# First feed-forward output layer: 18 instead of 16 of 22 hidden rows in seven-product pairs

## Chip, cores and metric

The kernel runs on one core of one Trainium2 chip. The metric is the device time of one execution in microseconds (us); lower is better. The engines named are TensorE (PE, matrix products), VectorE (DVE) and ScalarE (ACT) for elementwise work, GpSimd (POOL) for elementwise work off the matrix accumulators, and SyncE (SP), whose queue issues most of the DMA transfers. PSUM is the accumulator memory that PE writes; it is held here in banks named `mm` (four), `pn` (one) and `aux` (three).

## What is computed

The reference is one inference step of a one-layer decoder for 1024 prompt tokens and 8 sample tokens (1032 columns in the kernel, where activations stand transposed: features on the partitions, tokens along the row). The part that matters is the first of its two feed-forward networks and what follows it:

```python
def swiglu(x, wi, wo):
    g, u = jnp.split(x @ wi, 2, axis=-1)
    return (jax.nn.silu(g) * u) @ wo
...
x = layer_norm(ALPHA * x + 0.5 * swiglu(x, ffn1_wi, ffn1_wo), ln_g[0], ln_b[0])
z = x @ w_in + b_in
```

The model width is 1024, the hidden width 2816, that is 22 hidden rows of 128 features (pairs 0 to 10 of two rows). `ffn1_wo` is 2816 x 1024. A second network (`ffn2`), built by the same function with its own places, runs near the end.

## The kernel before

**Products.** Each float32 operand is split in two parts, high and low (`hilo`, `wload`, `wcomb`: a copy on ACT, then a subtraction on VectorE), and a product is three matmuls: high by high, high by low, low by high. A *plain* unit (`unit`, lines 172 to 174) makes one output tile of 128 features for one block of columns. A *seven-product* segment (`product`, lines 432 to 434) takes a 2 x 2 block product (two hidden rows by two output tiles, and the two halves of the columns) with seven products instead of eight; the sums that this needs of the weights (`wcomb`: two on VectorE, two on POOL) and of the activations are made beside the matmuls. The 1032 columns are two halves of 516, each in a part of 256 and one of 260: four blocks, numbered 0 to 3; blocks 0 and 2 have 256 columns, 1 and 3 have 260 (`BLK4`).

**Hidden layer.** `ffn` first makes pair 0 by plain units, then pairs 1 to 10 in seven products (`hidden`, `pair`). `spill` writes a pair to DRAM: for a pair that the output layer takes plainly, the two rows as they are (`hscr`); for one that it takes in seven products, the seven combinations of half-rows (`hsum`), for which it makes four sums on VectorE and four on POOL (lines 514 to 517).

**Output layer.** `groups` lists which pairs go together through the segments and, for each of the seven products, which places in SBUF hold their half-rows. For each group the half-rows are loaded from `hsum` by SP and split (`split_load`: cast on ACT, line 588; subtraction on VectorE, line 589); then four segments follow, one for each 256 output features. A segment loads its part of `ffn1_wo`, makes the seven weight combinations (lines 258 to 275), runs 7 products x 2 column parts x the group's pairs x 3 matmuls, and adds each product to the result rows `RT` (line 612, VectorE, from PSUM). Before: the groups are the pairs (1, 2, 3), (4, 5, 6) and (7, 8).

`plains` lists the rows that remain, each with two places. Before: rows 0, 1, 18, 19, 20, 21 (pairs 0, 9 and 10). Their activations come from `hscr` by the same `split_load`, the six 128 x 1024 weight rows by `wrow` in two halves (lines 148 and 149: cast on ACT, subtraction on VectorE) into 12 places: the nine of the weight ring and three `extra` ones.

**Tail and norm.** The plain rows are not multiplied at once. `tail1` only hands on the result rows and a function `last`, which the code after `ffn` calls for each block in the order 0, 2, 1, 3 and each of eight output tiles: one plain unit over all plain rows, then an addition to the result row (line 647, VectorE, high priority). `ln_sum` adds up the block on POOL (lines 369 and 371), and `ln_halves` makes the norm: a matmul with a matrix of 1/1024 for the mean (line 385), eight subtractions from PSUM on VectorE (390), eight squares on ACT (392), their sum on POOL and VectorE (396 to 404), a second matmul for the variance (407), the reciprocal root on ACT and its refinement on VectorE (409 to 412), then scale on VectorE (415), shift on ACT (417), and the high and low parts of the result (211 and 212). From the second block on, the first VectorE step queues behind the root of the block before. So each block's norm runs while PE makes the next block's units. Units take PSUM from `mm` and `pn` in turn, five in all.

After that the q and k projections are made by plain units for the four blocks in the same order, 96 matmuls a block, evicted by ACT (line 976). Meanwhile VectorE and POOL make the sums of x for the seven-product projections (lines 222 to 225, split at 211 and 212) and the first weight combinations, and the first pair of projections begins.

**Order.** Each engine works through its own queue in order. The order within a queue comes from the build: a scheduler takes the program's operations by priority and readiness, so moved places and other dependencies change the order in the queues too. A place in SBUF (numbers 0 to 35, the ring's names and `sreg`) is reused when all readers of its last content are done; a transfer into a place that isn't free waits at the head of SP's queue.

Of the kernel before, what the change touches and what calls it, by code (L numbers as in the profile page):

```python
# [63 lines left out]
def layer_kernel(ctx: ExitStack, tc: tile.TileContext, I, O):  # L64
# [12 lines left out]
    def gen(i, dt=F32, n=NT):  # L77

        tag = f"a{i}" if isinstance(i, int) else i
        return sb.tile([128, 1024 if tag in WN else 4 * BM], dt, name=tag, tag=tag)[:, :1024 if tag in WN else n]  # L80
# [56 lines left out]
    def set_ring(slots):  # L137
        ring["slots"] = slots
        ring["i"] = 0

    def wload(src, k, n, dst=None, raw=None, eng=None):

        if raw is None:
            raw = rawp.tile([128, 512], F32, name="raw", tag="raw")[:, :k * n]
            DQ.dma_start(raw.rearrange("p (k n) -> p k n", n=n), src)
        s = slot() if dst is None else dst
        hi, lo = s[:, :k * n], s[:, 512:512 + k * n]
        S.copy(hi, raw)
        (eng or V).tensor_tensor(lo, raw, F_(hi), op=OP.subtract)  # L149
        return hi.rearrange("p (k n) -> p k n", n=n), lo.rearrange("p (k n) -> p k n", n=n)  # L150
# [12 lines left out]
    def wrow(w, rows, half, dst=None):  # L163

        t = [wload(w[r:r + 128, half * 512:(half + 1) * 512].rearrange("p (k n) -> p k n", n=128), 4, 128,
                   gen(dst[i], R) if dst else None) for i, r in enumerate(rows)]
        return [[(hi[:, j, :], lo[:, j, :]) for hi, lo in t] for j in range(4)]
# [15 lines left out]
    def bs(t, b, blk=BLK):  # L183
        c0, n = blk[b]
        return t[:, c0:c0 + n]
# [95 lines left out]
    xscr = tc.dram_tile([8, 128, NT], F32, name="xscr")  # L281
# [202 lines left out]
    def ffn(wi, wo, l, XS, enter, xlate, raws, sgs, RTs, res, groups, plains, tail, extra=None):  # L484
# [99 lines left out]
        def split_load(t, src):  # L584

            hi, lo = t
            DQ.dma_start(F_(lo), src)
            S.copy(hi, F_(lo))
            V.tensor_tensor(lo, F_(lo), F_(hi), op=OP.subtract)  # L589
            return hi, lo  # L590
# [51 lines left out]
        def ounit(js, w, m, b, blk=BLK):  # L642
            ps = unit_ps(blk[b][1])
            unit(ps, w, cols([hid[j][0] for j in js], [hid[j][1] for j in js], b, blk))
            r = bs(RT[m], b, blk)
            with tc.high_priority():
                V.tensor_tensor(r, r, ps, op=OP.add)  # L647

        for gi, rows_ in enumerate(plains):
            js = [j for j, _ in rows_]  # L650
            for j, ss in rows_:
                hid[j] = split_load([gen(x, R) for x in ss], hscr[j])
            rows = [j * 128 for j in js]
            if gi < len(plains) - 1:
                for half in range(2):
                    ws = wrow(wo, rows, half)
                    for q in range(4):
                        for b in range(3):
                            ounit(js, ws[q], half * 4 + q, b)
            else:  # L660
                if extra:
                    r = ring["slots"][ring["i"] % 9:] + ring["slots"][:ring["i"] % 9]
                    set_ring(r)
                    ws = wrow(wo, rows, 0, r[0:5] + extra[0:1]) + wrow(wo, rows, 1, extra[1:] + r[5:])
                else:
                    ws = wrow(wo, rows, 0) + wrow(wo, rows, 1)
                tail(RT, lambda m, b, blk: ounit(js, ws[m], m, b, blk))
# [47 lines left out]
    def xlate1():  # L715
        tslot(X1[0], 0, (16, 20, 8, 12))
        tslot(X1[0], 1, (17, 21, 9, 13))
        for kp in range(4):
# [2 lines left out]

    G1 = [((1, 2, 3), (0, 1, 2, 3, 4, 5, 6, 7, 14, 15, 22, 23, 8, 9, 10, 11, 12, 13, 26, 27, 28)),
          ((4, 5, 6), (29, 34, 35, 0, 1, 2, 3, 4, 5, 6, 7, 14, 15, 22, 23, 8, 9, 10, 11, 12, 13)),
          ((7, 8), (34, 35, 26, 27, 28, 29, 0, 1, 2, 3, 8, 9, 10, 11))]
    T1 = [list(zip((0, 1, 18, 19, 20, 21), ((4, 5), (6, 7), (14, 15), (22, 23), (12, 13), (34, 35))))]
    RT1 = []

    def tail1(RT, last):
        RT1.extend(RT)
        RT1.append(last)  # L730

    ffn(I["ffn1_wi"][0], I["ffn1_wo"][0], 0, X1, enter1, xlate1, [30, 31, 32, 33], [14, 15, 34, 35],
        [16, 17, 24, 25, 18, 19, 20, 21], xscr, G1, T1, tail1, [28, 29, 33])


    w_in = I["w_in"][0]
# [753 lines left out]
    for m in range(8):  # L1490
        for b in range(3):
            ps = unit_ps(BLK[b][1])
            unit(ps, wa[m // 4][m % 4], cols(MH[:K2], ML[:K2], b))
            r = bs(r2[m], b)
            V.scalar_tensor_tensor(r, r, ALPHA, ps, op0=OP.mult, op1=OP.add)
    rows = [k * 128 for k in range(K2, 8)]
# [57 lines left out]
    def tail2(RT, last):  # L1554
# [3 lines left out]
        for b in range(4):  # L1558
# [14 lines left out]
          ((7, 8, 9), (30, 31, 32, 35, 4, 5, 0, 1, 6, 7, 2, 3, 28, 29, 33, 34, 10, 11, 12, 13, 25))]  # L1573
    T2 = [[(0, (14, 15))], [(1, (30, 31)), (20, (32, 33)), (21, (24, 25))]]
    ffn(I["ffn2_wi"][0], I["ffn2_wo"][0], 2, X2, enter2, xlate2, [16, 17, 26, 27], [33, 34, 8, 9],
        (21, 22, 23, 18, 19, 20, 8, 9), rscr, G2, T2, tail2)

# [252 lines left out]
```

## Time and profile before

| | us |
|---|---|
| median of three runs | 2691.29 (2688.82 to 2695.84) |
| profiled execution, whole | 2685.85 |
| its span, first to last instruction | 2684.0 |
| PE busy in the span | 2638.3 |
| VectorE busy | 1871.4 |
| ACT busy | 1287.8 |
| POOL busy | 652.8 |

The output layer of the first network begins at about 466 us of the span. The second group starts at 525, the third at 587; the tail's units begin at 624, the q and k units at 697, and the first projection pair at 745 us. A window row of the profile gives, for one stretch, its length, then the busy time of PE, weight loads, VectorE, ACT and POOL with the number of instructions after x, then the granted PE clock, the DMA share and the rate. A group row gives line, engine, operation, what it writes and reads, the count, the busy time and the mean of one in ns, and after the bar the idle time of the engine just before these instructions and who ended it. A waits row reads: who waited, for whom, us in total, how often, the longest.

### The profile page before, as it was taken

How to read it: one execution, taken by the hardware profiler on the slowest of the kernel's cores; microseconds unless marked ns; L12 is line 12 of the kernel's file. 1: busy time of each engine (PE TensorE's matmuls, PEld its weight loads, DVE VectorE, ACT ScalarE, POOL GpSimd, SP SyncE). 2: the span in 40 equal slices, each digit the busy share in tenths (PEclk: the TensorE clock that was granted, in tenths of full speed). 3: DMA queues.
4: the chain of work that ended last, by engine and by line, in shares of the span. 5: the costliest groups of instructions: out<-in, count | busy, mean ns of one | idle time of the engine just before them, and what ended most of it. 6: DMA issues, size and time to landing. Idle time of an engine off the chain costs nothing.

```text
span 2684.0 us, 56381 instructions
## 1 busy us (share of the span) xinstructions
PE 2638.3 (98%) x21775; PEld 2604.1 (97%) x21775; DVE 1871.4 (70%) x4124; ACT 1287.8 (48%) x2839; POOL 652.8 (24%) x648
## 2 busy tenths in 40 slices
PE   9999999999999999999999999999999999999998
PEld 9999999999999999999999999999999999999887
DVE  6755556997885756656666678658855555888887
ACT  5444446433554445446666555425544444543351
POOL 2222221112421111111111345323422222111454
PEclk9999999999999999999999999999999999999999
DMA  6333235432332434236657776821423323643211
GB/s 207 103 108 107 91 105 197 161 121 68 115 97 88 123 99 127 79 89 191 188 176 243 236 238 219 256 81 46 157 91 107 104 89 107 219 154 114 86 47 58
DMA packets 311924, 355.15 MB, mean 132 GB/s; under 512 B 28536, under 2 KB 246344, under 8 KB 311656
## 3 DMA queue, kind: packets, MB, share of 16 engines
q1 hardware_dynamic: 289336, 330.30, 38.7%
q10 hardware_dynamic: 22320, 21.26, 2.6%
q8 instruction: 170, 2.79, 0.4%
q14 instruction: 98, 0.80, 0.1%
HBM read 246.09 MB, written 105.42 MB: 131 GB/s over the span
## 4 chain that ended last, share of the span: by engine, by line
PE 79%; DVE 9%; DMA 5%; ACT 2%; issue 2%; POOL 1%; SPq 0%; ACTq 0%; DVEq 0%; POOLq 0%
PE mm L432 13%; PE mm L433 13%; PE mm L434 13%; PE aux L432 5%; PE aux L434 5%; PE aux L433 5%; PE mm L172 5%; PE mm L174 5%; PE mm L173 5%; PE pn L172 1%; PE pn L173 1%; PE pn L174 1%; DVE a L212 1%; DVE a L589 1%; DVE w L259 1%
## 5 line engine op out<-in xcount | busy, mean ns | idle before, releaser
L432 PE MATMUL mm<-a,w 128*128 128x260 f32 (+1 forms) x2313 | 654.9, 283 | 3.4 <-DVE a L612 2.5
L433 PE MATMUL mm<-a,w 128*128 128x260 f32 (+1 forms) x2313 | 651.0, 282 | 0.9 <-DVE a L212 0.9
L434 PE MATMUL mm<-a,w 128*128 128x260 f32 (+1 forms) x2313 | 649.9, 281 | 0.0
L432 PEld LDWEIGHTS mm<-a,w 128*128 128x128 f32 x2313 | 435.3, 188 | 9.0 <-issue 3.7
L433 PEld LDWEIGHTS mm<-a,w 128*128 128x128 f32 x2313 | 435.7, 188 | 1.5 <-DVE a L212 1.3
L434 PEld LDWEIGHTS mm<-a,w 128*128 128x128 f32 x2313 | 435.3, 188 | 0.1
L275 POOL TENSOR_TENSOR raw<-a,raw 128x512 f32<-128x512 f32 (+2 forms) x98 | 124.6, 1272 | 1149.1 <-issue 448.8
L259 DVE TENSOR_TENSOR w<-raw,w 128x512 fp32r<-128x512 f32 (+2 forms) x258 | 174.6, 678 | 189.5 <-ACT w L258 188.2
L432 PE MATMUL aux<-a,w 128*128 128x260 f32 (+1 forms) x1000 | 282.0, 282 | 1.8 <-DVE a L454 1.5
L433 PE MATMUL aux<-a,w 128*128 128x260 f32 (+1 forms) x1000 | 281.1, 281 | 0.0
L434 PE MATMUL aux<-a,w 128*128 128x260 f32 (+1 forms) x1000 | 281.1, 281 | 0.0
L432 PE MATMUL mm<-a,e 128*128 128x260 f32 (+1 forms) x785 | 222.5, 283 | 0.9 <-DVE a L612 0.6
L433 PE MATMUL mm<-a,e 128*128 128x260 f32 (+1 forms) x785 | 221.2, 282 | 0.7 <-DVE a L212 0.7
L434 PE MATMUL mm<-a,e 128*128 128x260 f32 (+1 forms) x785 | 220.8, 281 | 0.0
L174 PE MATMUL mm<-a,w 128*128 128x256 f32 (+3 forms) x739 | 208.0, 284 | 0.2 <-DVE w L149 0.2
L172 PE MATMUL mm<-a,w 128*128 128x260 f32 (+4 forms) x695 | 198.0, 286 | 3.2 <-DVE a L647 1.7
L173 PE MATMUL mm<-a,w 128*128 128x260 f32 (+4 forms) x695 | 197.0, 285 | 0.0
L258 ACT CAST w<-a 128x512 fp32r<-128x512 f32 (+2 forms) x200 | 117.2, 587 | 161.5 <-PE mm L434 95.3
L432 PEld LDWEIGHTS aux<-a,w 128*128 128x128 f32 x1000 | 188.2, 188 | 2.9 <-DVE a L454 2.0
L434 PEld LDWEIGHTS aux<-a,w 128*128 128x128 f32 x1000 | 188.2, 188 | 0.0
L433 PEld LDWEIGHTS aux<-a,w 128*128 128x128 f32 x1000 | 188.2, 188 | 0.0
L258 ACT CAST w<-raw 128x512 fp32r<-128x512 f32 (+2 forms) x258 | 152.2, 591 | 65.6 <-PE aux L434 21.6
(546 smaller groups left out, 7726.1 us busy)
## 6 DMA issues: line engine op xcount, KB each, us to landing
a<-in_ffn_wi_dram SPq DMA_DIRECT2D x80, 512.0 KB
a<-in_w_in_dram SPq DMA_DIRECT2D x68, 512.0 KB
a<-hsum SPq DMA_DIRECT2D x119, 258.0 KB
hsum<-a SPq DMA_DIRECT2D x68, 258.0 KB
a<-in_ffn_wo_dram SPq DMA_DIRECT2D x40, 384.0 KB
a<-in_state_C_dram ACTq DMA_DIRECT2D x32, 256.0 KB
out_dram<-a ACTq DMA_DIRECT2D x32, 256.0 KB
raw<-in_w_b_dram SPq DMA_DIRECT2D x32, 256.0 KB
```

Source lines behind the costliest of these rows:

```text
L172: T.matmul(ps, wh, xh, start=(i == 0), stop=False)
L173: T.matmul(ps, wh, xl, start=False, stop=False)
L174: last = T.matmul(ps, wl, xh, start=False, stop=(i == n - 1))
L212: order_["lo"] = V.tensor_tensor(dst[1], src, F_(dst[0]), op=OP.subtract).ins
L258: S.copy(hi, src)
L259: V.tensor_tensor(lo, src, F_(hi), op=OP.subtract)
L275: G.tensor_tensor(s4, a12, s2, op=OP.subtract)
L432: T.matmul(ps, wh, xh, start=start and kp == 0, stop=False, skip_group_check=True)
L433: T.matmul(ps, wh, xl, start=False, stop=False, skip_group_check=True)
L434: T.matmul(ps, wl, xh, start=False, stop=stop and kp == len(xs) - 1, skip_group_check=True)
L589: V.tensor_tensor(lo, F_(lo), F_(hi), op=OP.subtract)
```

## The change

Pair 9 (rows 18 and 19) goes from the plain rows to the third group, so that 18 rows go through seven products and four plain rows (0, 1, 20, 21) stay beside the norm. The third group's places are dealt anew for its 21 half-rows, and so are the plain rows' places. The eight weight rows of the tail take four places of the ring (its oldest) and four `extra` ones; the ring then starts after the four.

```diff
                 if extra:
                     r = ring["slots"][ring["i"] % 9:] + ring["slots"][:ring["i"] % 9]
-                    set_ring(r)
-                    ws = wrow(wo, rows, 0, r[0:5] + extra[0:1]) + wrow(wo, rows, 1, extra[1:] + r[5:])
+                    set_ring(r[4:] + r[:4])
+                    ws = wrow(wo, rows, 0, r[0:4]) + wrow(wo, rows, 1, extra)
...
-          ((7, 8), (34, 35, 26, 27, 28, 29, 0, 1, 2, 3, 8, 9, 10, 11))]
-    T1 = [list(zip((0, 1, 18, 19, 20, 21), ((4, 5), (6, 7), (14, 15), (22, 23), (12, 13), (34, 35))))]
+          ((7, 8, 9), (26, 27, 28, 34, 35, 29, 4, 5, 0, 22, 23, 1, 6, 7, 2, 14, 15, 3, 8, 9, 10))]
+    T1 = [list(zip((0, 1, 20, 21), ((12, 13), (34, 35), (4, 5), (22, 23))))]
...
     ffn(I["ffn1_wi"][0], I["ffn1_wo"][0], 0, X1, enter1, xlate1, [30, 31, 32, 33], [14, 15, 34, 35],
-        [16, 17, 24, 25, 18, 19, 20, 21], xscr, G1, T1, tail1, [28, 29, 33])
+        [16, 17, 24, 25, 18, 19, 20, 21], xscr, G1, T1, tail1, [33, 6, 7, 14])
```

`spill` takes its choice for pair 9 from the same table `T1`, so that pair is now written as seven half-row combinations. The second network is not touched; its own tables already have pairs (7, 8, 9) as a third group, with one plain row ahead of the tail and three beside its norm.

## Prediction before the run

> **What bounds the kernel now.** I read the page first (engine shares, then the chain that ended last), then the first network's output layer by stages, then who made TensorE (PE) wait there, then VectorE (DVE) by form.
>
> ```profile
> span 2684.0 us, 56381 instructions
> PE 2638.3 (98%) x21775; PEld 2604.1 (97%) x21775; DVE 1871.4 (70%) x4124; ACT 1287.8 (48%) x2839; POOL 652.8 (24%) x648
> PE 79%; DVE 9%; DMA 5%; ACT 2%; issue 2%; POOL 1%; SPq 0%; ACTq 0%; DVEq 0%; POOLq 0%
> ```
>
> TensorE is busy nearly throughout and holds 79% of the chain. So a matmul taken away is worth its issue interval, and a wait on VectorE is worth its whole length. The stages (PE, weight loads, DVE, ACT, POOL; matmuls after x):
>
> ```profile
> core 0: us, PE busy (x) PEld busy (x) DVE busy (x) ACT busy (x) POOL busy (x), PEclk, DMA share, GB/s
> 465.80:525.40 59.60, 59.60 (x504) 59.60 (x504) 54.20 (x119) 29.79 (x56) 9.12 (x8) 1.00 0.58 193
> 587.00:607.00 20.00, 18.50 (x143) 17.54 (x144) 20.00 (x51) 6.39 (x15) 2.86 (x4) 1.00 0.10 33
> 2427.00:2447.00 20.00, 18.76 (x151) 18.00 (x151) 20.00 (x46) 6.38 (x12) 2.23 (x2) 1.00 0.27 80
> 623.90:645.80 21.90, 21.90 (x186) 21.74 (x185) 12.84 (x28) 4.97 (x8) 5.13 (x6) 1.00 0.43 121
> 645.80:697.10 51.30, 51.30 (x424) 51.03 (x423) 42.58 (x100) 26.02 (x65) 25.18 (x29) 1.00 0.09 22
> 697.10:744.80 47.70, 47.19 (x392) 46.81 (x391) 42.58 (x93) 31.09 (x82) 21.82 (x17) 1.00 0.50 167
> ```
>
> The first row is the first group of three pairs: 504 matmuls in 59.60 us, no gap, so one matmul costs 59.60/504 = 0.1183 us (the 0.28 us that the page gives a matmul overlaps its neighbours). The next two rows are the first 20 us of the third group, in the first network (two pairs) and the second (three pairs, as the change makes the first): VectorE is 100% busy in both, and PE gets 143 and 151 of the 169 matmuls that 20 us hold. The last three rows are the tail up to the first norm, the rest of the tail, and the q/k stage up to the first projection pair. PE is full there; VectorE has slack, 13.8 us in the last two stages together.
>
> ```profile
> engine line waited for: us in total, times, longest us
> PE mm L432 <- DVE a L612: 2.0, 4, 0.8
> PE mm L433 <- DVE a L212: 0.7, 1, 0.7
> PE aux L407 <- DVE a L404: 0.5, 1, 0.5
> PE pn L432 <- DVE a L612: 0.3, 1, 0.3
> PE aux L432 <- DVE a L612: 0.2, 1, 0.2
> ```
>
> These are all waits of PE from 455 to 770 us: group changes (L612), the last norm's variance matmul (L407), the transformed x of the first projection pair (L212). The same answer for the second network's tail (2502.5 to 2610 us), which has only three rows beside its norm:
>
> ```profile
> PE aux L407 <- DVE sreg L404: 3.0, 1, 3.0
> PE mm L172 <- DVE a L647: 1.7, 3, 0.8
> PE mm L172 <- ACT a L211: 0.7, 1, 0.7
> ```
>
> **The change part by part.** *Matmuls.* A plain row pair costs 2 rows x 8 output tiles x 4 column blocks x 3 = 192 matmuls; in seven products 4 segments x 7 x 2 column parts x 3 = 168. Net -24 x 0.1183 = **-2.8 us**: the tail loses 192 matmuls (22.7 us), the third group gains 168 (19.9 us).
>
> *Change from second to third group.* With three pairs the third group should start as the second network's does: 151 matmuls where the first network now has 143, 8 x 0.1183 = **-0.9 us**. The bounds are 0 and -3.1 (all 26 missing matmuls).
>
> *Preparing the third group's operands, off PE.*
>
> ```profile
> L589 DVE TENSOR_TENSOR a<-a 128x516 fp32r<-128x516 f32 x19 | 14.2, 759 | 1.1 <-ACT a L588 1.1
> L589 DVE TENSOR_TENSOR a<-a,a 128x1032 fp32r<-128x1032 f32 x5 | 6.1, 1219 | 0.0
> L259 DVE TENSOR_TENSOR w<-raw,w 128x384 fp32r<-128x384 f32 x10 | 5.4, 546 | 0.0
> L259 DVE TENSOR_TENSOR w<-raw,w 128x256 fp32r<-128x256 f32 x10 | 4.1, 412 | 0.0
> ```
>
> VectorE gets 7 more half-row splits (7 x 0.759 = 5.3) and 28 wider weight splits (28 x 0.134 = 3.8), and loses two whole-row splits (2 x 1.219 = 2.4): +6.7 us, beside 19.9 us more of matmuls. Per matmul the group gets lighter for VectorE; that is why I take a gain above. Pair 9's four extra sums each on VectorE and POOL, and its seven more stores, fall in the hidden layer, as they already do for pairs 1 to 8, beside matmuls and on engines that the first fence shows 70% and 24% busy: nothing. If that cover were gone, it would be four block-wide sums of about 0.42 us (the form of L647 below), 1.7 us.
>
> *Moved places: the last plain row's load.* Its slots come free after product 3 of the last segment; products 4 to 6 (54 matmuls) and rows 0, 1, 20 of the first tail unit (9) then cover 63 x 0.1183 = 7.5 us. Now the last such load went
>
> ```profile
> 618.04 0.33 SPq L587 DMA_DIRECT2D a<-hscr  x1
> 621.32 1.05 ACT L588 CAST a<-a 128x1032 fp32r<-128x1032 f32 x1 [0.87 <-DMA a<-hscr]
> 623.23 1.22 DVE L589 TENSOR_TENSOR a<-a,a 128x1032 fp32r<-128x1032 f32 x1
> ```
>
> from issue to the end of its split in 623.23 + 1.22 - 618.04 = 6.4 us. It fits by 1.1 us: 0, at most +1 if queued behind a weight split. The wait on SP's queue holds back the wo rows' loads behind it, ACT's its casts; both feed the same tail start. The eight wo rows find their slots in the order in which they are loaded, the last (14) after product 5, four output tiles before it is used: 0.
>
> *The norm's cover.* This is the open term. The norm of each block runs on VectorE, ACT and POOL behind the next block's matmuls. Its mean matmuls now stand at
>
> ```profile
> 646.90 0.59 PE L385 MATMUL aux<-a,onesm 128*128 128x256 f32 x2
> ...
> 667.08 0.59 PE L385 MATMUL aux<-a,onesm 128*128 128x256 f32 x2
> ...
> 686.87 0.60 PE L385 MATMUL aux<-a,onesm 128*128 128x260 f32 x2
> ...
> 701.94 0.60 PE L385 MATMUL aux<-a,onesm 128*128 128x260 f32 x2
> ```
>
> 20.2, 19.8 and 15.1 us apart: the first two steps are set by PE's 144 matmuls a block (17.0 us), the last shows that a norm can follow in 15.1 us or less. With 96 matmuls (11.4 us) a block they would have to follow faster, or fall behind, until the q/k stage (96 matmuls a block as well) needs their result. Before the first mean there are 576 - 414 = 162 tail matmuls (424 less five norm pairs of 2 leaves 414 after it); it would be 96 + 18 = 114. So 48 matmuls (5.7 us) go ahead of the first norm and 144 (17.0 us) go out of the stretch from it to the first projection pair, which takes 51.30 + 47.70 = 99.0 us and holds 42.58 + 42.58 = 85.2 us of VectorE. The end therefore moves by 19.9 - 5.7 - 0.9 = +13.3 plus (stretch - 99.0):
> - PE alone sets it, no wait: stretch 99.0 - 17.0 - 0.5 = 81.5, end **-4.2**;
> - VectorE sets it and never idles: 85.2, end **-0.5**;
> - VectorE sets it and keeps the idle time that others than PE cause it (below), 92.4: **+6.7**;
> - no shrinking at all: **+13.3**.
>
> I price the waits between the two known tails, in proportion to rows beside the norm (six now, three in the second network): the variance matmul 0.5 with six, 3.0 with three, so 2.2 with four; the PSUM evictions (L647) 0 and 1.7, so 1.1; the first pair's x sums stay near their 0.7 but start later, +0.5 (0 to +4, by what VectorE lacks). From the -4.2 that is +2.2 + 1.1 + 0.5 = +3.8, **sum -0.4, call it -0.5**, and this agrees with the second bound. Some slack exists: the first pair runs 48 matmuls (5.7 us) before it needs the x sums.
>
> *Sum.* -2.8 - 0.9 + (2.2 - 0.5) + 1.1 + 0.5 = -0.4 to -0.5. The profiled execution took 2685.85 us (span 2684.0 and 1.85 around it) and would take 2685.3; the runs' median, 2691.29, is 5.4 above it, so the median becomes **2690.8 us**.
>
> **Rivals.** *VectorE becomes the bound in the norm (slower).* What speaks for it is its own idle time by who caused it, in the 99.0 us:
>
> ```profile
> L647 DVE TENSOR_TENSOR a<-a,mm 128x260 f32<-128x260 f32 x13 | 5.3, 415 | 0.9 <-PE mm L174 0.8
> L410 DVE TENSOR_TENSOR a<-a 128x256 f32<-128x256 f32 x2 | 0.9, 426 | 3.2 <-ACT a L409 3.2
> L212 DVE TENSOR_TENSOR a<-tmp,a 128x256 fp32r<-128x256 f32 x16 | 6.9, 454 | 1.3 <-ACT a L211 1.3
> L149 DVE TENSOR_TENSOR w<-raw,w 128x512 fp32r<-128x512 f32 x5 | 4.7, 947 | 1.2 <-ACT w L148 1.2
> L222 DVE TENSOR_TENSOR tmp<-a 128x256 f32<-128x256 f32 x4 | 2.1, 527 | 1.5 <-POOL a L398 1.5
> L412 DVE SCALAR_TENSOR_TENSOR a<-a 128x256 f32<-128x256 f32 x2 | 1.6, 801 | 0.1
> L412 DVE SCALAR_TENSOR_TENSOR a<-a 128x260 f32<-128x260 f32 x2 | 0.9, 426 | 0.0
> ```
>
> 3.2 + 1.3 + 1.2 + 1.5 = 7.2 us come from ACT and POOL, not PE, so 85.2 + 7.2 = 92.4: 2698.0; with no shrinking 2704.6. It decides once a block's norm costs VectorE and its suppliers more than a block's matmuls. Against it: the second network's three-row tail lost 1.7 + 3.0 + 0.7 us, not ten. Chance 0.15.
>
> *VectorE and POOL collide more.* The last two rows are one operation, at 801 ns while POOL was adding and at 426 ns while it was not; L647, which reads PSUM, stays at 415. L212 at 454 and L222 at 527 ns are in between. Against 415 these three rows lose 2 x 0.386 + 16 x 0.039 + 4 x 0.112 = 1.8 us in 22 instructions, so at most 16 us in the 193 that the two windows count. POOL's 25.18 + 21.82 = 47.0 us squeezed from 99.0 into 81.5 us meet VectorE 1.2 times as often: at most 16 x 0.2 = 3.2 us; as many of the 193 read PSUM, I take half, +1.6: 2692.4. The Trainium skill's page "SBUF — State Buffer", section "SBUF: two separate sides", says that the two engines take a shared port pair as an exclusive lock for a whole instruction when VectorE has two SBUF inputs and GpSimd reads SBUF, which would make this rival's sign certain; the 801 and 426 ns agree. Chance 0.10.
>
> *All these waits go.* The third group then loses none of its 26 matmuls and neither norm nor first pair waits: -2.8 - 3.1 - 0.5 - 0.7 = -7.1, 2684.2. Against it: VectorE is short by 85.2 - 81.5 = 3.7 us. Chance 0.12.
>
> *Row pair not moved out of the tail*, because other code still takes it as plain: the two tables agree, so 0.03, 2691.3.
>
> **How the numbers follow.** The forecast keeps 0.60: 2690.8, its own range 2687 (no wait at all, -4.2) to 2694 (x sums at +4 instead of +0.5). A measurement of this kernel tells about 0.3% (8.1 us) from no change. Faster by more: half of the last gain case, whose 7.1 us fall just short, and 0.02 of the forecast: 0.08. Slower by more: two thirds of the first rival and 0.03 of the rest: 0.13. Within: 0.79. The range reaches from the gain case, 2684, to just past the first rival's lower price, 2699.
>
> **What would show it.** PE's matmul count falls by 24. The third group's first 20 us hold about 151 matmuls. The mean matmuls stand 13 to 16 us apart. VectorE is over 95% busy from the first norm to the first projection pair; waits of PE on L404, L647 and L212 total 3 to 6 us between 600 and 770 us. I am wrong if that sum is over 10 us, if the steps stay at 20 us, or if a wait on L588/L589 appears at the tail's start; and if time changes elsewhere, where nothing was edited, my stage account missed it.

## The result: 7 us slower, and in the profiles only a third of it where the edit is

The changed kernel takes 2699.87 us (median of 20 runs, 2692.91 to 2704.40) against 2693.09 us of the kernel before, measured beside it (20 runs). The ratio is 1.0026, 95% interval 1.0019 to 1.0033: +7.0 us. A second measurement of the same two gave 1.0028 (1.0018 to 1.0038). The forecast was 2690.8 us in a range that ended at 2699, so the time lies just outside it. By the bound of 0.3% the change is still "within", but the interval leaves no doubt of the sign, and it is not the sign of the sum (-0.4 to -0.5).

The profile after, first from the page:

```profile
span 2692.6 us, 56366 instructions
PE 2639.3 (98%) x21751; PEld 2605.8 (97%) x21751; DVE 1882.1 (70%) x4129; ACT 1288.2 (48%) x2840; POOL 653.0 (24%) x652
```

PE has 24 matmuls less and nearly the same busy time; the span is 8.6 us longer. Where? The next table takes an instruction of VectorE that both kernels have, and the difference of its start to its start in the first profile of before; it shows what each stretch adds to that difference. Two profiles of each kernel stand side by side, because one alone misleads (which instruction is taken near a border moves an entry by up to 0.5 us): the second profile of the unchanged kernel is itself 5.8 us behind the first one.

| us | before, first | before, again | after, first | after, again |
|---|---|---|---|---|
| 0 to 500 | 0 | -0.1 | +1.6 | +0.1 |
| 500 to 800 (third group, tail, q/k, first pair) | 0 | +0.5 | **+2.2** | **+2.1** |
| 800 to 1200 | 0 | +0.1 | -0.6 | -0.9 |
| 1200 to 1400 | 0 | +0.5 | **+2.9** | **+4.2** |
| 1400 to 1820 | 0 | +4.5 | +3.5 | +3.4 |
| 1820 to 1960 (second norm, second network's entrance) | 0 | -0.9 | **+1.5** | **+0.9** |
| 1960 to 2680 | 0 | +1.3 | -2.5 | -1.3 |

Three stretches set the two kernels apart: the edited stage by about 1.9 us, 1200 to 1400 us by about 3.3, the second network's entrance by about 1.7. What 1400 to 1820 us seems to add, the unchanged kernel adds too when it runs again; and part of what the last row seems to give back is a stretch at half clock near 2570 us, which both profiles of before have, the first of after has not, and the second of after has for 3.4 us where the second of before has 6.8.

**The edited stage.** The four mean matmuls of the norm, the tail with the q/k stage from the first of them to the first projection pair, and who made PE wait from 455 to 780 us:

```profile
662.41 0.60 PE L385 MATMUL aux<-a,onesm 128*128 128x256 f32 x2
...
674.56 0.60 PE L385 MATMUL aux<-a,onesm 128*128 128x256 f32 x2
...
691.33 0.60 PE L385 MATMUL aux<-a,onesm 128*128 128x260 f32 x2
...
709.96 1.07 PE L385 MATMUL aux<-a,onesm 128*128 128x260 f32 x2
```
```profile
662.41:747.10 84.69, 82.12 (x661) 81.13 (x660) 80.21 (x179) 53.05 (x141) 38.30 (x44) 0.98 0.27 90
```
```profile
engine line waited for: us in total, times, longest us
PE aux L407 <- DVE a L404: 1.9, 1, 1.9
PE mm L432 <- DVE a L612: 1.6, 3, 0.8
PE mm L433 <- DVE a L212: 1.4, 2, 0.9
PE pn L432 <- DVE a L612: 1.3, 2, 1.0
PE mm L432 <- ACT sreg L457: 0.7, 1, 0.7
PE mm L173 <- DVE sreg L212: 0.6, 1, 0.6
```

The means now stand 12.2, 16.8 and 18.6 us apart: the second block follows nearly at PE's pace (96 matmuls, 11.4 us), the third and fourth more slowly. VectorE is busy 80.21 of 84.69 us (95%). The stretch has shrunk from 98.0 us (646.90 to 744.86) to 84.7. The one long wait is for the sum of squares (L404). What stands ahead of it, on GpSimd and on VectorE:

```profile
696.97 2.71 POOL L398 TENSOR_TENSOR a<-a,tmp 128x260 f32<-128x260 f32 x3
...
702.45 4.32 POOL L371 TENSOR_TENSOR a<-a,a 128x260 f32<-128x260 f32 x5
...
702.80 4.24 DVE L212 TENSOR_TENSOR a<-a,a 128x256 fp32r<-128x256 f32 x5
...
708.32 0.42 DVE L404 TENSOR_TENSOR a<-a,tmp 128x260 f32<-128x260 f32 x1
```

GpSimd's part of that sum (L398) has ended at 699.7 us, 8.6 us ahead of L404. So L404 waits for its turn on VectorE, which shows no idle time from 686 us to there; five splits (L212) shortly ahead of it take 4.24 us beside GpSimd's additions (L371). What follows the wait is in the timeline and in the windows of 3.41 us on both sides of it (length, then PE, weight loads, VectorE, ScalarE, GpSimd, and the granted clock third from the end):

```profile
706.57 0.28 PE L173 MATMUL pn<-a,w 128*128 128x256 f32 x1
708.79 0.70 PE L407 MATMUL aux<-a,onesm 128*128 128x260 f32 x2 [1.95 <-DVE a L404]
709.14 0.47 PE L174 MATMUL pn<-a,w 128*128 128x256 f32 x1
```
```profile
706.20:709.61 3.41, 1.46 (x11) 1.21 (x10) 3.21 (x8) 0.07 (x1) 0.57 (x1) 1.00 0.18 53
709.61:713.02 3.41, 3.41 (x17) 3.22 (x16) 2.99 (x9) 1.72 (x5) 0.48 (x1) 0.50 0.14 38
```

For 3.41 us behind the pause PE runs at half clock: 17 matmuls where 29 would fit. So the wait costs its 1.95 us and, by estimate, 3.41/2 = 1.7 us more.

**Order.** Instruction by instruction, each engine's order is that of before but for pair 9's sums in the hidden layer (near 430 us) and in two places: the edited stage, and 1150 us later the end of the second norm with the second network's entrance, where no line was edited. There VectorE now takes more splits of the first weights (L149) ahead of a norm block's own steps: its reciprocal root's refinement (L410) starts 7.1 us behind its sum of squares (L404), where it was 4.2.

### The profile page after: what moved, and what is told of

Same layout as the page of the kernel before. It is cut to its first block, busy times and chain, and to the rows that moved or that the text cites. A ratio compares the mean times of both kernels' runs of the same rounds, so it can differ in the third digit from the quotient of the medians.

```text
span 2692.6 us, 56366 instructions
## 1 busy us (share of the span) xinstructions
PE 2639.3 (98%) x21751; PEld 2605.8 (97%) x21751; DVE 1882.1 (70%) x4129; ACT 1288.2 (48%) x2840; POOL 653.0 (24%) x652
## 4 chain that ended last, share of the span: by engine, by line
PE 79%; DVE 9%; DMA 6%; ACT 3%; issue 2%; POOL 1%; SPq 0%; ACTq 0%; DVEq 0%; POOLq 0%
PE mm L432 14%; PE mm L433 14%; PE mm L434 14%; PE aux L432 6%; PE aux L434 6%; PE aux L433 6%; PE mm L172 5%; PE mm L174 5%; PE mm L173 5%; DVE a L212 2%; PE pn L172 1%; PE pn L173 1%; PE pn L174 1%; DMA a<-in_w_in_dram 1%; DVE w L259 1%
## 5 line engine op out<-in xcount | busy, mean ns | idle before, releaser
L432 PE MATMUL mm<-a,w 128*128 128x256 f32 (+1 forms) x2359 | 667.7, 283 | 3.5 <-DVE a L612 1.8
L433 PE MATMUL mm<-a,w 128*128 128x256 f32 (+1 forms) x2359 | 664.6, 282 | 1.9 <-DVE a L212 1.8
L434 PE MATMUL mm<-a,w 128*128 128x256 f32 (+1 forms) x2359 | 662.8, 281 | 0.0
L432 PEld LDWEIGHTS mm<-a,w 128*128 128x128 f32 x2359 | 444.4, 188 | 8.2 <-issue 2.3
L433 PEld LDWEIGHTS mm<-a,w 128*128 128x128 f32 x2359 | 444.8, 189 | 2.9 <-DVE a L212 2.8
L434 PEld LDWEIGHTS mm<-a,w 128*128 128x128 f32 x2359 | 444.3, 189 | 0.1
L275 POOL TENSOR_TENSOR raw<-a,raw 128x512 f32<-128x512 f32 (+1 forms) x98 | 126.9, 1295 | 1142.1 <-issue 514.1
L259 DVE TENSOR_TENSOR w<-raw,w 128x512 fp32r<-128x512 f32 (+1 forms) x262 | 177.9, 681 | 187.6 <-ACT w L258 185.8
L432 PE MATMUL aux<-a,w 128*128 128x256 f32 (+1 forms) x988 | 278.4, 282 | 2.8 <-DVE a L454 2.7
L433 PE MATMUL aux<-a,w 128*128 128x256 f32 (+1 forms) x988 | 277.8, 281 | 0.0
L434 PE MATMUL aux<-a,w 128*128 128x256 f32 (+1 forms) x988 | 277.8, 281 | 0.0
L432 PE MATMUL mm<-a,e 128*128 128x256 f32 (+1 forms) x782 | 221.2, 283 | 1.4 <-DVE tmp L470 0.8
L434 PE MATMUL mm<-a,e 128*128 128x256 f32 (+1 forms) x782 | 220.0, 282 | 0.0
L433 PE MATMUL mm<-a,e 128*128 128x256 f32 (+1 forms) x782 | 220.0, 281 | 0.0
L172 PE MATMUL mm<-a,w 128*128 128x260 f32 (+3 forms) x689 | 198.4, 289 | 5.9 <-ACT w L148 2.7
L258 ACT CAST w<-a 128x512 fp32r<-128x512 f32 (+1 forms) x196 | 115.7, 591 | 167.4 <-PE mm L434 100.1
L174 PE MATMUL mm<-a,w 128*128 128x260 f32 (+4 forms) x683 | 194.5, 286 | 0.1
L258 ACT CAST w<-raw 128x512 fp32r<-128x512 f32 (+1 forms) x262 | 156.0, 596 | 77.1 <-PE aux L434 24.2
```

Of the source, the lines that this page charges most:

```text
L172: T.matmul(ps, wh, xh, start=(i == 0), stop=False)
L174: last = T.matmul(ps, wl, xh, start=False, stop=(i == n - 1))
L258: S.copy(hi, src)
L259: V.tensor_tensor(lo, src, F_(hi), op=OP.subtract)
L275: G.tensor_tensor(s4, a12, s2, op=OP.subtract)
L432: T.matmul(ps, wh, xh, start=start and kp == 0, stop=False, skip_group_check=True)
```

## The experiments

Each kernel ran in five rounds beside the kernel before. Three runs show how far ratios scatter when the work stays about the same: the repeat of before, a few idle matmuls and nine idle stores gave 1.0000, 1.0001 and 0.9989. A difference of 0.1% is not to be read as one.

Theory S: the loss is all made in the edited stage. Theory O: the stage costs 2 us, the rest comes from the changed order at the second entrance.

**Repeats.** No edit.

> The kernel before, unchanged, a second time: its ratio to itself shows how far two measurements of one program differ, and its profile how far the time of one place differs between two executions. The traces of before and after part by 1.6 us in the first 61 us and by 5 to 7 us between 800 and 1720 us, where both issue the same instructions in the same order. If that is variation between executions, this profile stands as far from the first one at those places, and the ratio is 1.000 within 0.001. If the parting belongs to the change, this profile repeats the first one within 1 us everywhere.

> The changed kernel a second time: the ratio was 1.0026 (1.0019 to 1.0033), so +7 us; expected again +5 to +9 us. At 708.8 us its profile should again show PE waiting about 2 us for VectorE's sum of squares (L404) and then matmuls at half the clock for some 3.4 us; if that was chance, the wait is below 1 us this time.

Measured: 1.0000 (0.9992 to 1.0009) and 1.0028. The 1.6 us at the start and the 4.5 us from 1400 to 1820 are the executions' variation; what the table shows in bold came in both profiles of after and in neither of before. The wait of 2 us for L404 and the half clock came again (at 707 us).

**Names only.** Before and after with the nine ring places (line 322) taken in another order:

```
-    set_ring(RING)
+    set_ring(RING[4:] + RING[:4])      # before
+    set_ring(RING[5:] + RING[:5])      # after
```

> The kernel before with the nine ring places taken in rotated order from the start: same work, same order everywhere but behind the second norm, at the second network's entrance, where the build puts VectorE's, ScalarE's and GpSimd's instructions in the order that the changed kernel has there. Theory S (all of the +7 us is made in the first network's last stage): 0, ratio 1.000. Theory O (that stage costs 2 us, and the reordered second entrance the rest): +5 us, ratio 1.0019.

> The changed kernel with the ring rotated the other way, so that the places and the order behind the first network's last stage, the second network's entrance among them, are those of the kernel before. Theory S: +7 us as the changed kernel, ratio 1.0026. Theory O: +2 us, ratio 1.0007.

Measured: 1.0027 (1.0018 to 1.0037) and 1.0021 (1.0012 to 1.0030). The first is remarkable: the kernel before, with nothing but names changed, is as slow as the changed one, and in its profile 4.4 us lie at the second entrance. Theory S had 1.000 for it and falls. The build's order there hangs on the places' names: in the kernel before with the ring rotated by four, the four engines' order differs there and nowhere else. The change shifts the ring by four places, and so it came to reorder instructions that it does not touch. Who PE waits for there (1820 to 1990 us), in before, after, and before with other names:

```profile
PE aux L407 <- DVE a L404: 0.2, 1, 0.2
```
```profile
PE mm L432 <- ACT sreg L457: 1.4, 1, 1.4
PE aux L407 <- DVE a L404: 1.2, 1, 1.2
PE aux L385 <- DVE a L371: 0.5, 1, 0.5
```
```profile
PE aux L407 <- DVE a L404: 1.8, 2, 1.4
PE mm L432 <- ACT sreg L450: 1.1, 1, 1.1
```

Over all profiles of this study but the one that edits this place itself, the stretch 1820 to 1960 us adds -1.6 to 0 us in the nine with the old order and +0.9 to +4.4 in the eight with the new one, 2.7 us between the means. But the second run refutes theory O as I had put it: with the old order back (-1.0 us there) the changed kernel is still 5.6 us slow. Renaming costs some 0.7 us of its own between 140 and 500 us in both; the cause stays open.

**The ring not rotated.**

```
-                    set_ring(r[4:] + r[:4])
+                    set_ring(r)
```

> The changed kernel with the ring left as it stood when the last row pairs' weights are loaded, not rotated by four places: the q/k weights then find their places only behind the tail, as in the kernel before, and not ahead of the norm; and, since the names of the places run as before, the build puts the second network's entrance in the old order again. The first network's ring is untouched, unlike in the two runs with renamed places. Theory S (the shortened cover of the norm costs all of the +7 us, whatever the ring does): +7 us, ratio 1.0026. Theory O (shortened cover 1 to 2 us, the rest from the reordered second entrance): +1 to +2 us, 1.0005. Theory Q (the five q/k weight splits that now run ahead of the norm, 5 x 0.95 = 4.7 us of VectorE, make the norm late): the wait for the sum of squares falls from 1.95 us to below 1, and the ratio is 1.000 or below.

Measured: 1.0035 (1.0022 to 1.0048), 9.4 us. The second entrance has the old order (-1.1 us), but the edited stage now costs 5.9 us: the weights come late and the norm is no earlier, and in place of L404 PE waits for the last block's splits:

```profile
PE mm L172 <- ACT sreg L211: 2.5, 1, 2.5
PE mm L433 <- DVE a L212: 1.5, 2, 1.2
PE aux L385 <- DVE a L371: 0.9, 1, 0.9
```

Theory Q falls; in the edited stage the rotation is worth keeping (2.1 us with it, 5.9 without).

**The cover given back.** The tail's first two rows multiplied twice:

```
-            unit(ps, w, cols([hid[j][0] for j in js], [hid[j][1] for j in js], b, blk))
+            unit(ps, w + w[:len(js) - len(w)], cols([hid[j][0] for j in js], [hid[j][1] for j in js], b, blk))
-                tail(RT, lambda m, b, blk: ounit(js, ws[m], m, b, blk))
+                tail(RT, lambda m, b, blk: ounit(js + js[:2] if extra else js, ws[m], m, b, blk))
```

> The changed kernel whose tail multiplies its first two rows twice (their contribution counts twice in the result, everything else is computed as in the changed kernel): 192 matmuls of 0.118 us more beside the norm, 22.7 us, and nothing more on VectorE. If the shortened cover gave nothing back, the time rises by the full 22.7 us over the changed kernel (ratio to before 1.011). If the norm was late under four rows by the 5 us that the traces show (matmul-free time 16.9 against 11.7 us from 440 to 800 us), it rises by 17 to 18 us (ratio to before 1.009): no wait for L404 over 0.7 us, and no stretch at half clock.

Measured: 1.0064 (1.0051 to 1.0077), +17.2 us over before, so about 10 over the changed kernel for 22.7 us of matmuls. Against before it has 168 matmuls more, 19.9 us, so 17.2 (13.7 to 20.7 by the interval) leaves no loss to be seen, behind the stage either. In its profile the stage adds 17.0 us where the changed kernel adds 2.1: 14.9 for 22.7. Of the other 7.8 us, 4.6 are the waits for L404, L212 and L457 shown above and 1.7 the half clock; PE waits for nothing between 640 and 800 us here, and the 16 splits (L212, 128 x 256) are back at 434 ns. The window from the first mean to the first pair shows PE busy without a break, and VectorE with 15 us of room:

```profile
666.48:763.56 97.08, 97.08 (x805) 96.63 (x804) 81.96 (x187) 54.67 (x142) 42.16 (x46) 1.00 0.25 83
```

So the two halves of the change are known apart: the third group costs 19.3 us up to the first mean (666.48 - 0.3 - 646.90; foreseen 19.9 - 0.9 = 19.0) and 17.0 with the stage behind it, where this run also lacks before's waits of 0.5 and 0.7 us; and the shorter tail gives back 14.9 of its 22.7.

**Weights of the second entrance held back.**

```
-                    if len(wp) < 4:
-                        wp.append(wcol(wi, k * FF + i * 128, raws=early.pop(0) if early else ()))
+                    with tc.issue_after(order_["rstd"]) if l else nullcontext():
+                        wp.extend([wcol(wi, k * FF + i * 128, raws=early.pop(0) if early else ())] if len(wp) < 4 else [])
```

> The changed kernel, with the second network's first weights held back until the last block's norm factor is made, so that VectorE splits them behind the norm's squares and not among them. First network's tail as in the changed kernel. Theory O: the wait for the sum of squares at the second entrance falls from 1.2 us to 0.2, its matmuls start without one, and the time falls by 2 to 5 us, ratio to before 1.001 to 1.002. Theory S: no difference, 1.0026. A wait for these weights may take the place of the one removed.

Measured: 1.0072 (1.0058 to 1.0087). It made things worse, by a wait in the place of the removed one: the weights now come too late, so PE has no unit to run between the mean and the variance matmul, and L407 waits for 12 us. Who PE waits for at that place:

```profile
PE aux L407 <- DVE a L404: 12.1, 1, 12.1
PE pn L174 <- DVE w L149: 2.5, 1, 2.5
```

It says that this place is sensitive, not which order is right; the runs with the old order say that.

**Two of eight splits to GpSimd** (in the first norm alone):

```
-            hilo(xplain(X7, c, m), bs(rows[m], c, BLK4))
+            hilo(xplain(X7, c, m), bs(rows[m], c, BLK4), G if m in (3, 7) and any(X7 is u for u in XP_[0] or ()) else V)
```

> The changed kernel with the low parts of two of the eight normed rows taken by GpSimd instead of VectorE (8 of 32 splits of 0.45 us, 3.6 us). If VectorE's work is what the four-row tail waits for, the waits for L404 and L212 shrink and the time falls by 2 to 3.6 us, ratio to before 1.0013 to 1.0019. If it is collisions between VectorE and GpSimd, GpSimd's 8 x 0.9 us more beside it give nothing or cost 1 us more: 1.0026 to 1.003.

Measured: 1.0040 (1.0028 to 1.0052). Slower, although VectorE has less to do: the stage adds 3.8 us instead of 2.1, and the 128 x 256 splits that stayed on VectorE take longer yet (12 of them, mean 861 ns; 757 in the changed kernel). This pointed to collisions.

**A delay alone**, in the kernel before:

```
-    wp = []
+    wp = warm(16) or []
```

> The kernel before with nothing changed but 16 small matmuls of about 0.27 us each (their result is read by nobody) ahead of the q/k stage's last part: everything behind them is 4 us later, in the old order. Theory R (the part of the loss that lies behind the edited stage comes from what is there, whatever shifts it: how its waits fall on transfers and on the clock): clock drops and longer waits appear between 1220 and 1800 us as in the changed kernel, and the time rises by 7 us, ratio 1.0026. Theory N (those are the executions' own variation): the time rises by the 4 us alone, 1.0015.

Measured: 1.0001 (0.9992 to 1.0010). The matmuls take 3.7 us and make what follows 2 us later, and nothing more is lost behind them (-0.1 us from 1200 to 1400). Theory R falls; theory N's 1.0015 was too much as well.

**Order in the norm, and places.** First the one, then the other, then both:

```
-        with tc.issue_after(order_["rstd"]) if b else nullcontext():
+        with tc.issue_after(order_["rstd"]) if b else nullcontext(), tc.high_priority() if l == 0 else nullcontext():
```
```
-                    set_ring(r[4:] + r[:4])
-                    ws = wrow(wo, rows, 0, r[0:4]) + wrow(wo, rows, 1, extra)
+                    set_ring(r)
+                    ws = wrow(wo, rows, 0, extra) + wrow(wo, rows, 1, r[5:9])
```

> The changed kernel with the subtraction, squares and sums of a block's norm ahead of the transformed rows (L212) of the block before in VectorE's order, in the first norm alone; the same instructions, only their order. If the order makes L404 late, its wait of 1.95 us falls below 1, the half clock behind it goes, and the time falls by 2 to 3.5 us: ratio to before 1.0014 to 1.002. If it is the sum of VectorE's work, the wait moves to L212 at the first projection pair and the time stays, 1.0026.

> The changed kernel with the tail's weights placed so that the first five q/k weights still find free places ahead of the norm, but the ring goes on as in the kernel before; the second network's entrance is then in the old order, and no place of the first network's other stages is renamed. Theory O: the edited stage costs 1.7 us as in the changed kernel, and the second entrance's 2 us are saved: ratio 1.0019. A wait for the tail's first weights, whose last place comes free only behind product 5, may take its place (up to 2 us).

> The two edits before this together: norm's sums first, and the old order at the second entrance. If both terms are real and independent, 2 to 3.5 us and 2 us are saved of the +7 us: ratio 1.0006 to 1.0012. If what remains behind the edited stage is untouched by either, 1.0015 or more.

Measured: 1.0023 (1.0013 to 1.0032), 1.0027 (1.0015 to 1.0039), 1.0007 (0.9997 to 1.0018). The norm's sums first: no gain that can be told alone, and L404 is waited for 2.4 us, so neither half of what was expected came. The places: the second entrance is back at -1.6 us, but the edited stage loses 8.6 us, 4.6 of them in a wait for the last block's split. PE's waits there, in the run with other places:

```profile
PE mm L172 <- ACT sreg L211: 4.6, 1, 4.6
PE mm L173 <- DVE a L212: 2.2, 1, 2.2
```

Together the stage adds 2.8 us, the second entrance -1.2, and the time cannot be told from before. It is the best version with the pair moved that computes the whole norm; none beats before.

**As many transfers as after**, in the kernel before:

```
-                return
+                return [DQ.dma_start(spare[k], sg[k % 2][:, 0:128]) for k in range(9 if p == 9 and not l else 0)]
```

> The kernel before with nine more small stores (128 x 128, into a place that nobody reads) on SyncE's queue at the end of the first hidden layer, so that as many transfers have been issued from that queue afterwards as in the changed kernel (1193 issues in the trace instead of 1184). Theory C (the number of transfers issued before sets where later issues stall): ScalarE's second issue at the state's first load takes about 3 us as in the changed kernel, not 0.4; the wait of PE for L454 near 1230 us is over 2 us, not 1.1 to 1.3; and the time rises by 2 to 4 us, ratio 1.001. If the count has no part in it, all three stay as they were and the ratio is 1.000.

Measured: 0.9989 (0.9980 to 0.9997); none of ScalarE's issues between 1180 and 1420 us takes over 1.5 us, and L454 is waited for 1.2 us at most. Theory C falls.

**Weights' splits on GpSimd**, with the norm's sums first, and then with the other places too (`wcol` hands `eng` on to `wload`):

```
-                    wp.append(wcol(w_in, (Q0, K0)[k] + i * 128))
+                    wp.append(wcol(w_in, (Q0, K0)[k] + i * 128, eng=G))
```

> The kernel with the norm's sums first, and the low parts of the eight q/k weights taken by GpSimd instead of VectorE (8 x 0.9 us of VectorE's work less in the tail; nothing of the norm waits for them). If VectorE's amount of work is what the four-row tail waits for, the waits for L404 and L212 fall by half or more and the time falls by 2 to 4 us from 1.0023, to 1.0010. If GpSimd's longer work on the norm's sums, which then stand behind the weights, makes the norm late instead, it stays or rises.

> The same with the places that give the second network's entrance its old order: norm's sums first, weights on GpSimd, old order. If the edited stage is then held by PE alone (-4.2 us by matmuls), it is faster than the kernel before: -2 to -4 us, ratio 0.9988. If one wait only takes the place of the other, it stays at the 1.0007 of the version without GpSimd's part or above.

Measured: 1.0023 (1.0014 to 1.0033) and 1.0020 (1.0011 to 1.0029); the stage adds 3.9 and 5.5 us. Eight weight splits taken off VectorE bring nothing when they go to GpSimd.

**Fewer sums on GpSimd.**

```
-            ln_sum(s1, rp, m, b, BLK4)
+            ln_sum(s1, rp, m, b, BLK4) if m in (1, 7) else None
-                    G.tensor_tensor(s2, s2, t, op=OP.add)
+                    G.tensor_tensor(s2, s2, t, op=OP.add) if l else None
```

> The changed kernel with GpSimd's sums in the first norm cut: of the eight rows only the first two and the last are added for the mean, and of the squares those of rows 2 to 4 are left out (8 of GpSimd's 10 additions a block go, so mean and variance are not the reference's). VectorE's instructions are the same. If VectorE is late because its two-operand instructions stand still beside GpSimd's, the transformed rows (L212, 128 x 256) fall from 757 ns to below 500, VectorE's work in the stage falls by 5 us or more, the wait of 1.95 us for L404 goes and with it the half clock, and the edited stage gives back 2 to 4 us: ratio 1.0011 to 1.0020. If it is VectorE's number of instructions, the means stay at 700 ns or the waits stay, and the ratio is 1.0026.

Measured: 1.0004 (0.9993 to 1.0015), 6 us less than the changed kernel, with VectorE's instructions the same. The stage adds **-2.6** us where the changed kernel adds +2.1. From the first mean to the first pair:

```profile
661.33:742.49 81.16, 80.22 (x662) 79.56 (x661) 70.97 (x179) 52.64 (x141) 16.12 (x17) 1.00 0.28 94
```

The stretch has the changed kernel's 179 VectorE instructions, and VectorE is busy 70.97 us with them instead of 80.21. Its groups in that stage by form (mean ns after the comma), in before, in after and in this run:

```profile
L415 DVE SCALAR_TENSOR_TENSOR a<-a,pc,a 128x256 f32<-128x256 f32 x16 | 6.5, 478 | 0.1
L212 DVE TENSOR_TENSOR a<-a,a 128x256 fp32r<-128x256 f32 x16 | 6.1, 428 | 0.0
...
L390 DVE TENSOR_TENSOR a<-a,aux 128x256 f32<-128x256 f32 x16 | 5.5, 414 | 2.3 <-PE aux L385 2.3
```
```profile
L212 DVE TENSOR_TENSOR a<-a,a 128x256 fp32r<-128x256 f32 x16 | 11.6, 757 | 0.0
...
L415 DVE SCALAR_TENSOR_TENSOR a<-a,pc,a 128x256 f32<-128x256 f32 x16 | 8.0, 568 | 0.0
...
L390 DVE TENSOR_TENSOR a<-a,aux 128x256 f32<-128x256 f32 x16 | 5.5, 413 | 0.6 <-PE aux L385 0.6
```
```profile
L415 DVE SCALAR_TENSOR_TENSOR a<-a,pc,a 128x256 f32<-128x256 f32 x16 | 6.6, 480 | 0.0
...
L212 DVE TENSOR_TENSOR a<-a,a 128x256 fp32r<-128x256 f32 x16 | 6.3, 424 | 0.0
...
L390 DVE TENSOR_TENSOR a<-a,aux 128x256 f32<-128x256 f32 x16 | 5.6, 415 | 0.6 <-PE aux L385 0.6
```

The same 16 splits take 428 ns in before, 757 in after, 424 with fewer GpSimd sums; the subtractions that read PSUM (L390) stay at 413 to 415 throughout. PE's wait for L404 is gone and no half clock follows. Record by record, 13 of the 16 splits in after overlap a GpSimd addition and take 620 to 970 ns; the three that do not take 411. In before eight overlap one, and only one of them is longer than 420 ns (630), so an overlap alone does not make a split late. This run takes away GpSimd's own time as well as the collisions; which share each has in the 6 us was not measured apart. But the 333 ns a split are VectorE's own time, and VectorE's queue is what L404 waited in. The Trainium skill, page "SBUF — State Buffer", section "SBUF: two separate sides", says that a VectorE operation with two SBUF inputs and a GpSimd operation that reads SBUF take a shared port pair one after the other, each for a whole instruction; these rows agree, L390 with its one SBUF input included.

## Why the prediction was wrong, step by step

**Matmuls, -2.8:** right in number (21751).

**Second to third group, -0.9:** the first mean stands 13.9 and 13.7 us later than before once the start's 1.6 and 0.1 us are taken off (662.41 - 1.63 - 646.90); the sum had 19.9 - 5.7 - 0.9 = 13.3. So 0.3 to 0.5 of the 0.9 was left by the first mean, though the third group's first 20 us hold 158 matmuls (159 in the repeat) where 151 were foreseen. No wait on L588 or L589 at the tail's start: the operands and places cost nothing, as foreseen.

**The stretch:** foreseen 81.5 + 3.8 = 85.3 us, counted from 645.80 us; between the ends that are measured here (98.0 us in before) that is 84.3, measured 84.7 and 84.8. Right in size, with VectorE at just under 95% and with 3.9 us of waits for L404, L647 and L212 where 3 to 6 were foreseen. But the means stand 12 to 19 us apart, not 13 to 16, and the size did not come by the terms named: the wait for L404 was 1.9 (2.2 foreseen), the evictions cost nothing (1.1 foreseen), and the half clock, 1.7, had no term at all. The x sums behind it were sized too small: L212 and L457 hold PE for 1.4 + 0.7 + 0.6 = 2.7 us in the last q/k matmuls and the first pair, where 1.2 was foreseen (0.7 and 0.5 more). So the stage ends at +2.1 instead of -0.5.

**The rival "VectorE and POOL collide more"** had the sign and the mechanism, and too small a size. It scaled the losses of before with the overlap, 1.2 times, and got at most 3.2 us, priced at 1.6. Like for like, the 156 VectorE instructions of those groups that have the same count in four windows are busy 71.3 us in before, 75.1 in after, 71.9 with the cover given back and 66.5 with fewer sums (added up from the rows by form). So the shorter cover costs 3.8 us more of VectorE's time; what of the end that is alone was not measured. The 4.7 us between the stage with the sums (+2.1) and without (-2.6) are something else, the price of nearly all of GpSimd's sums in the changed kernel. The kernel before met such collisions too (its L404 took 946 ns and its L412 801 in the blocks of 256 columns) and had the slack for them; in after they fell on the splits ahead of L404. Without the sums the stretch is 81.2 us, close to the bound "PE alone sets it", which is 80.5 between the same ends.

**The step that failed most** is the *Sum* itself, in two ways. First, it took a wait as worth its own length and had no term for the clock. Every run has its granted clock: 0.9959 in the mean of the ten runs of the repeat, 0.9977 in the 29 of before measured beside them. (1 - clock) x span, taken as time lost, is 11.0 us against 6.1, so by this estimate up to 4.9 of the 7.5 us between the two means are half clock, and not only the 1.7 behind L404. The runs split by it: 5.4 to 6.6 us in all that keep the pair where it was, 6.5 with the cover given back, 8.3 with fewer sums, and 9.4 to 19.4 in all others with the pair moved. New names alone cost 7 us with no clock lost (6.0), so that is a loss of another kind.

Second, -0.4 to -0.5 came from a stage account that ended at the first projection pair, and everything behind was set to zero without a term. The prediction's last sentence named this way to be wrong, and it gave no price. Behind it lie, in the profiles, some 5 us: at the second entrance 1.7 by the two pairs of profiles (2.7 by all), through an order that the build chose by names; and about 3.3 between 1200 and 1400 us. There the instructions and their order are those of before. Two waits of PE from 1215 to 1380 us, in before and in after:

```profile
PE pn L1203 <- DVE tmp L1207: 1.8, 1, 1.8
PE aux L432 <- DVE a L454: 1.1, 1, 1.1
```
```profile
PE pn L1203 <- DVE tmp L1207: 2.4, 1, 2.4
PE aux L432 <- DVE a L454: 2.3, 1, 2.3
```

Each is 0.6 to 1.2 us longer, and one of them brings a half clock (1296.7 us; in the repeat 1232.8). In before's repeat they are 0.4 us and three waits of at most 1.2, without a half clock. Over the study this stretch adds -0.1 to +1.0 us in the five profiles without the moved pair and -1.1 to +10.8 in the thirteen others, 3.6 in the mean. The source **stays open**: it is not a delay of 2 us alone, not the number of transfers, not names alone (before with other names adds 1.0 there). With the cover given back the stretch adds nothing in the one profile. In after, its repeat and some others ScalarE's second issue of a state load takes about 3 us instead of 0.4, but in others with the same loss it does not.

## What to carry to other kernels

Moving matmuls from one place to another is not worth their difference when an engine works behind them: here 22.7 us of them gave 14.9 when taken away, because the cover that was left was too short for what VectorE and GpSimd do beside it. Before adding up such a move, squeeze the slower engine's work into the new stretch at the duration that it has *beside* its neighbour (here 757 or 801 ns, not 428), give a wait of about 2 us a chance of another 1.7 for the clock, and compare the granted clock over all runs, not in one profile. Where the build orders instructions itself, compare the order of the whole program before and after: a shift of place names alone moved this kernel by 7 us.

## What the runs showed of the hardware

The half clock comes on a fixed grid. Its starts in after, 709.61, 1296.70 and 1716.54 us, lie 172 and 295 times 3.4133 us from the first. What decides is how empty the grid's window was before it. Two windows of after ahead of a half clock, then the two on which the norms-first run's pause of nearly the same kind (2.6 us from matmul to matmul) fell:

```profile
1293.29:1296.70 3.41, 0.97 (x9) 0.81 (x8) 3.22 (x9) 2.25 (x6) 0.00 (x0) 1.00 0.20 51
...
1713.13:1716.54 3.41, 0.75 (x7) 0.54 (x5) 2.06 (x7) 0.62 (x1) 3.09 (x4) 1.00 1.07 338
```
```profile
702.27:705.68 3.41, 1.59 (x14) 1.38 (x12) 3.41 (x5) 1.60 (x5) 3.03 (x4) 1.00 0.26 77
705.68:709.09 3.41, 2.88 (x22) 2.82 (x23) 3.34 (x10) 0.86 (x2) 0.00 (x0) 1.00 0.00 0
```

With PE busy 1.46 us (above), 0.97 or 0.75 of 3.41 the next window ran at half clock; with 1.59 it did not, since the grid cut that pause in two. Over all profiles the border lies about half: windows at full clock that were under 44% busy were followed by it, those from 44 to 55% partly, those over 55% never. A window that itself ran at half clock was followed by another even at up to 78% (before's repeat, 2571.0 us). The Trainium skill, page "TensorE: Matmul & The Clock Gate", section "What's actually happening", gives a free-running window of 3413 ns and the half rate after an idle one. The length and the free running agree; here a window that PE was busy for 43% of is enough. So the same pause costs 1.7 us more in one execution than in the next, which is part of why single profiles of one kernel stand 6 us apart.
